# Strassen's seven products for the up projections of both token halves, with the gate products kept in HBM

## The chip, the cores and the metric

One core of a Trainium2 chip runs one program. The metric is the device time of one execution in microseconds (us); the time before is the median of three runs. The engines are named as in the profile: PE (TensorE, matmuls), DVE (VectorE), ACT (ScalarE), POOL (GpSimd) and SP (SyncE, whose queue issues all transfers here).

## The reference

Two post-norm layers over 1024 tokens of width 1024, in float32. Layer 0 has a mixer of gated MLP and sparse attention, layer 1 a convolution module; behind each comes the same kind of feed-forward part, which this change is about:

```
def conv_ffn(x, w_up, conv_w, conv_b, w_down):
    h = causal_dwconv(x @ w_up, conv_w, conv_b)
    g, u = jnp.split(h, 2, axis=-1)
    return (jax.nn.gelu(g) * u) @ w_down
...
x <- LayerNorm(alpha * x + f(x))        # behind every part
```

`w_up` is 1024 x 5632 (2816 gate and 2816 up columns), the convolution is causal with width 3, `w_down` is 2816 x 1024. Layer 1's mixer is `x @ w_in` (to 2 x 1024), a sigmoid gate, a causal depthwise convolution of width 31, LayerNorm, swish and `@ w_out`.

## The kernel before

Float32 accuracy comes from splitting each operand into a high and a low part in the fast matmul type; a product is three matmuls (`mm3`: high x low, low x high, high x high). `split` and `wload` make the parts: ACT copies the high part, POOL (for weights) or DVE subtracts it for the low one. Each weight tile of 512 KB comes on SP's queue into one of three buffers and is split into three buffers each.

The tokens are in two halves of 512 (h = 0, 1). `ffn(h, l)` does one half of layer l: 22 pairs of a gate tile and an up tile of 128 columns. `up(j)` makes one pair: for each tile eight k-chunks of three matmuls of 128 x 128 by 512 tokens; ACT takes the bias and the newest tap from PSUM, DVE the two older taps (for h = 1 also a correction from the first half's last tokens, `hal` and `cor`), ACT the gelu, POOL the product of gate and up, and the product is split again and stays in SBUF. Behind 8, 8 and 6 pairs come the down projections (`product`, tokens in rows, weights in blocks of two k-rows), which `into` adds to Z on DVE.

Python generators set the order of the program: each `yield` ends a unit of PE work of 24 matmuls (5.44 us), and `go(gen, n, rate)` emits n units and, behind each, `rate` waiting steps of the depthwise convolution's taps (`pump`). Such a tap is one DVE instruction per 128 channels and 512 tokens, 30 per tile, accumulated in one of two PSUM buffers (tag "c"). `mix` puts units of another stream behind the short steps of a norm. So `norm(0, g1)`, `conv_in(0)` and the taps of one half lie beside the other half's feed-forward units. `norm` takes the inverse root (`rsqrt`, eleven small DVE steps) for each token tile alone, transposes on PE and splits. `conv_norm` transposes, normalizes and transposes back. The framework then orders each engine's instructions by when their inputs are expected.

Of the kernel before, what the change touches and what calls it, by code (L numbers as in the profile page):

```python
# [18 lines left out]
T = 1024  # L19
# [6 lines left out]
F2W = 256  # L26

# [10 lines left out]
def trunk_kernel(ctx, tc, xt, wab, wv, w280, wst, sgub, sgulg, sgulb, pe_k, pe_v, w1k, w1v, w2k, w2v,  # L38
# [37 lines left out]
    def mm3(out_, ah, al, bh, bl, first, last):  # L76
        nc.tensor.matmul(out_, ah, bl, start=first, stop=False)  # L77
        nc.tensor.matmul(out_, al, bh, start=False, stop=False)  # L78
        nc.tensor.matmul(out_, ah, bh, start=False, stop=last)  # L79
# [40 lines left out]
    # the first two weights come in halves, between the first parts of x  # L120
# [207 lines left out]
    VT = kp.tile([128, 8, 2, 2, 128], F32R, name="VT")  # key tile, sel/win, group, (hi|lo)  # L328
# [41 lines left out]
    def product(lhs, src, kn, done, banks=None):  # L370
        # tokens in rows: blocks of two rows of weights, four token tiles side by side
# [53 lines left out]
    def late(qi):  # L425
        # the first half's output projection starts behind the last units of attention
# [18 lines left out]
    pe_.close()  # L445
    ps = es.enter_context(pool("ps1", space=PSUM))
    with pool("att") as tp:
# [4 lines left out]
        def tables_of(h, m):  # L452
# [18 lines left out]
        def front(u):  # L471
# [11 lines left out]
            # probabilities of the two heads: selected, window, compressed  # L483
# [9 lines left out]
            for e in range(2):  # L493
# [15 lines left out]
                # where the keys begin in the two banks, and how many of them the first bank takes  # L509
# [34 lines left out]
        def back(u):  # L544
# [6 lines left out]
            # transposed probabilities, and their products with the values  # L551
# [88 lines left out]
    def norm(h, gb):  # L640
# [23 lines left out]
    hal = fp.tile([128, 44, 2], F32, name="halo")  # L664
    cor = fp.tile([128, 44, 2], F32, name="cor")

    def ffn(h, l, tail=None):
        xh, xl = XT[h]
        z = Z[h]
        cw = V[f"fw{l}"].rearrange("p (m k) -> p m k", k=3)  # L670
        cb = f"fb{l}"
        if h == 1:
            cor2 = tmp("cor2")[:, :44]
            nc.vector.tensor_tensor(cor[:, :, 0], hal[:, :, 1], cw[:, :, 1], op=OP.mult)
            nc.vector.tensor_tensor(cor2, hal[:, :, 0], cw[:, :, 0], op=OP.mult)
# [30 lines left out]
        def down_last(tail):  # L706
            # the last product of all, one token tile after the other, with its weights kept
# [21 lines left out]
        def down(gi):  # L729
            j0, j1 = KG[gi]  # L730
            return product(lambda k: prod[j0 + k], lambda dh, b: wdn[l, gi * 8 + dh * 4 + b], j1 - j0,
                           into(h, gi == 0, gi == 2))

        done = 0
        for gi, (j0, j1) in enumerate(KG):
            top = min(j1 + 1, NPAIR)
            if tail and gi == 2:
                last = down_last(tail)
            while done < top:
                for _ in up(done):  # L740
                    yield
                    if tail and gi == 2 and done < 20:
# [247 lines left out]
```

## Time and profile before

| | |
|---|---|
| time, median of 3 runs | 2356.73 us (2356.02 to 2357.6) |
| span of the profiled execution, first to last instruction | 2353.9 us |
| instructions | 30312 |
| PE busy | 2299.9 us, 98% |
| DVE, ACT, POOL busy | 1318.5, 955.4, 1347.8 us |
| moved by DMA | 232.23 MB |

The span is one execution, taken by the hardware profiler; the median lies 2.8 us above it, which is around the span. Lines L61 and on are lines of the kernel. Matmuls overlap in PE, so their busy times are a union and their mean durations are longer than what each adds.

### The profile page before, as it was taken

How to read it: one execution, taken by the hardware profiler on the slowest of the kernel's cores; microseconds unless marked ns; L12 is line 12 of the kernel's file. 1: busy time of each engine (PE TensorE's matmuls, PEld its weight loads, DVE VectorE, ACT ScalarE, POOL GpSimd, SP SyncE). 2: the span in 40 equal slices, each digit the busy share in tenths (PEclk: the TensorE clock that was granted, in tenths of full speed). 3: DMA queues.
4: the chain of work that ended last, by engine and by line, in shares of the span. 5: the costliest groups of instructions: out<-in, count | busy, mean ns of one | idle time of the engine just before them, and what ended most of it. 6: DMA issues, size and time to landing. Idle time of an engine off the chain costs nothing.

```text
span 2353.9 us, 30312 instructions
## 1 busy us (share of the span) xinstructions
PE 2299.9 (98%) x10959; PEld 1915.2 (81%) x10959; DVE 1318.5 (56%) x2628; ACT 955.4 (41%) x1594; POOL 1347.8 (57%) x1277
## 2 busy tenths in 40 slices
PE   9999899999999999999999999999999999999998
PEld 7888798887788888788888887788888887888887
DVE  3532898657422223779983546789961739423325
ACT  4133998733433333333333442334243532433341
POOL 4442777554666656555566563655566664665672
PEclk9999999999999999999999999999999999999999
DMA  7053121353232232223332232233223233333240
GB/s 232 30 150 88 51 64 53 115 184 99 90 99 92 96 99 99 81 90 98 99 96 94 89 108 90 90 99 99 94 94 99 81 117 117 108 99 98 93 140 36
DMA packets 82989, 232.23 MB, mean 99 GB/s; under 512 B 10079, under 2 KB 24039, under 8 KB 82840
## 3 DMA queue, kind: packets, MB, share of 16 engines
q1 hardware_dynamic: 82840, 230.30, 30.7%
q8 instruction: 87, 1.43, 0.2%
q14 instruction: 62, 0.51, 0.1%
HBM read 213.44 MB, written 8.43 MB: 94 GB/s over the span
## 4 chain that ended last, share of the span: by engine, by line
PE 85%; DVE 11%; ACT 1%; issue 1%; DMA 1%; POOL 0%; DVEq 0%; SPq 0%; ACTq 0%; POOLq 0%
PE pu L77 13%; PE pu L79 13%; PE pu L78 13%; PE pd L77 8%; PE pd L79 8%; PE pd L78 8%; PE pt L563 2%; DVE Z L636 2%; DVE Z L637 1%; PE pca L79 1%; PE pcg L79 1%; PE pcg L77 1%; PE pca L77 1%; PE pcg L78 1%; PE pca L78 1%; PE O L571 1%
## 5 line engine op out<-in xcount | busy, mean ns | idle before, releaser
L73 POOL TENSOR_TENSOR wl<-wraw,wh 128x512 fp32r<-128x512 f32 x680 | 883.4, 1321 | 777.7 <-ACT wh L70 763.5
L77 PE MATMUL pu<-XTl,wh 128*128 128x512 f32 x1440 | 566.2, 393 | 14.2 <-DVE nw L616 4.1
L78 PE MATMUL pu<-XTh,wl 128*128 128x512 f32 x1440 | 564.5, 392 | 0.0
L79 PE MATMUL pu<-XTh,wh 128*128 128x512 f32 x1440 | 564.4, 392 | 0.0
L70 ACT ACTIVATE wh<-wraw 128x1024 fp32r<-128x1024 f32 x340 | 357.9, 1054 | 425.3 <-PE pd L79 362.7
L689 DVE SCALAR_TENSOR_TENSOR acc<-pu,vec,acc 128x511 f32<-128x511 f32 x176 | 131.7, 748 | 440.4 <-ACT acc L688 428.3
L77 PEld LDWEIGHTS pu<-XTl,wh 128*128 128x128 f32 x1440 | 272.4, 189 | 73.4 <-issue 15.2
L767 DVE SCALAR_TENSOR_TENSOR cacc<-ht,vec,cacc 128x512 f32<-128x512 f32 x464 | 318.6, 750 | 5.5 <-ACT cacc L763 3.9
L79 PEld LDWEIGHTS pu<-XTh,wh 128*128 128x128 f32 x1440 | 272.4, 189 | 56.9
L78 PEld LDWEIGHTS pu<-XTh,wl 128*128 128x128 f32 x1440 | 272.7, 189 | 56.1
L688 ACT ACTIVATE acc<-pu,vec 128x512 f32<-128x512 f32 x176 | 137.1, 779 | 423.5 <-PE pu L79 423.2
L77 PE MATMUL pd<-wl,ph 128*128 128x512 f32 x656 | 259.4, 396 | 0.8 <-DVE Z L398 0.4
L78 PE MATMUL pd<-wh,pl 128*128 128x512 f32 x656 | 258.9, 395 | 0.0
L79 PE MATMUL pd<-wh,ph 128*128 128x512 f32 x656 | 256.9, 395 | 0.0
L77 PEld LDWEIGHTS pd<-wl,ph 128*128 128x128 f32 x656 | 123.6, 188 | 31.3 <-DVE Z L398 2.0
L79 PEld LDWEIGHTS pd<-wh,ph 128*128 128x128 f32 x656 | 123.5, 188 | 28.6
L78 PEld LDWEIGHTS pd<-wh,pl 128*128 128x128 f32 x656 | 123.7, 188 | 28.4
L398 DVE TENSOR_TENSOR Z<-Z,pd 128x512 f32<-128x512 f32 x64 | 43.7, 685 | 178.9 <-PE pd L79 178.9
L690 DVE SCALAR_TENSOR_TENSOR acc<-pu,vec,acc 128x510 f32<-128x510 f32 x176 | 131.5, 747 | 4.6
L396 DVE SCALAR_TENSOR_TENSOR Z<-Z,pd 128x512 f32<-128x512 f32 x64 | 43.7, 684 | 158.4 <-PE pd L79 158.4
L699 POOL TENSOR_TENSOR acc<-acc 128x512 f32<-128x512 f32 x88 | 113.6, 1291 | 17.6 <-DVE acc L694 14.6
L63 POOL TENSOR_TENSOR pl<-acc,ph 128x512 fp32r<-128x512 f32 x88 | 113.7, 1292 | 11.9 <-ACT ph L62 9.6
(256 smaller groups left out, 3849.0 us busy)
## 6 DMA issues: line engine op xcount, KB each, us to landing
wraw<-wup SPq DMA_DIRECT2D x176, 512.0 KB, 3.4
wraw<-wdn SPq DMA_DIRECT2D x82, 512.0 KB, 3.4
wraw<-cwin SPq DMA_DIRECT2D x32, 512.0 KB, 3.4
wraw<-wout SPq DMA_DIRECT2D x16, 512.0 KB, 4.4
wraw<-cwout SPq DMA_DIRECT2D x16, 512.0 KB, 3.5
wraw<-wab SPq DMA_DIRECT2D x14, 512.0 KB, 3.8
gb<-lns SPq DMA_DIRECT2D x12, 512.0 KB, 3.6
B<-fd SPq DMA_DIRECT2D x8, 512.0 KB, 3.6
```

Source lines behind the costliest of these rows:

```text
L63: (leng or nc.vector).tensor_tensor(lo, src, hi.bitcast(F32), op=OP.subtract)
L70: nc.scalar.activation(wh[:, :n], raw[:, :n], AF.Copy)
L73: (leng or nc.gpsimd).tensor_tensor(wl[:, c], raw[:, c], wh[:, c].bitcast(F32), op=OP.subtract)
L77: nc.tensor.matmul(out_, ah, bl, start=first, stop=False)
L78: nc.tensor.matmul(out_, al, bh, start=False, stop=False)
L79: nc.tensor.matmul(out_, ah, bh, start=False, stop=last)
L563: nc.tensor.transpose(pt[:, j, e * 128:(e + 1) * 128], P[:, e, o:o + kn], ident)
L688: nc.scalar.activation(a, p, AF.Identity, scale=cw[:, mt, 2:3], bias=col(cb, mt))
L689: nc.vector.scalar_tensor_tensor(a[:, 1:], p[:, :511], cw[:, mt, 1:2], a[:, 1:], op0=OP.mult, op1=OP.add)
L690: nc.vector.scalar_tensor_tensor(a[:, 2:], p[:, :510], cw[:, mt, 0:1], a[:, 2:], op0=OP.mult, op1=OP.add)
L699: nc.gpsimd.tensor_tensor(acc[0], acc[0], acc[1], op=OP.mult)
L767: nc.vector.scalar_tensor_tensor(c[0] if k else ht[:, :H], ht[:, k:k + H], dww[:, j, k:k + 1], c[0], op0=OP.mult, op1=OP.add)
```

## The change

The up projection of a pair is taken as a 2 x 2 block product: rows are the gate tile and the up tile, the 1024 inputs are two halves of 512, and the tokens are two halves of 512. Strassen's form (in Winograd's variant) makes it from seven products of 512 inputs by 512 tokens where the plain form has eight. The sums of token blocks (T1 to T4) are made once per layer (`sums`), those of the weight blocks per pair (`prep`). `block` runs the seven products on two PSUM tiles of two banks; three of them accumulate onto banks that ACT or DVE has read in between, and DVE adds the rest. Taps, gelu and product then run over 1024 tokens.

A layer now has three stages. `up_lead` makes the first 4 pairs (layer 0) or 8 pairs (layer 1) in the old form, half by half; `up_rest` makes the second half's lead and then the other pairs by `block`; every product goes to HBM (`pd`). Then `down(0, l)` and `down(1, l)` fetch the products back, split them and run the down projections. The normalized tokens are written to HBM (`zd`) by `norm` and fetched back as Z. `norm` takes one inverse root for all four token tiles. Three of the sixteen depthwise tiles (`POOLED`) have their taps as an ACT multiplication and a POOL addition. Layer 0's second down projection and the lead tiles of layer 1 now lie beside the convolution's parts.

```
+LEAD = (4, 8)
+NP = 23
+POOLED = ((0, 3), (1, 1), (1, 3))
...
+    def mm3(out_, ah, al, bh, bl, first, last, more=False):
+        nc.tensor.matmul(out_, ah, bl, start=first, stop=False, skip_group_check=more)
+        nc.tensor.matmul(out_, al, bh, start=False, stop=False, skip_group_check=more)
...
+    keep = ctx.enter_context(pool("keep"))
+    hal = keep.tile([128, 2 * max(LEAD), 2], F32, name="halo")
+    cor = keep.tile([128, 2 * max(LEAD), 2], F32, name="cor")
+    pd = [[tc.dram_tile([128, 1024], F32, name=f"pd{l}_{j}") for j in range(NPAIR)] for l in range(2)]
+    zd = [tc.dram_tile([2, 128, 4, 1024], F32, name=f"zd{l}") for l in range(2)]
...
+    def ptile(dtype, name, w=512):
+        return fa.tile([128, w], dtype, name=name, tag="p", bufs=NP)
...
+    def norm(h, gb, keep=None):
         xh, xl = XT[h] = A("xh", F32R, name="XTh"), A("xl", F32R, name="XTl")
+        mv = fp.tile([128, 4, 2], F32, name="mv4", bufs=2)
+        for tt in range(4):
+            nc.vector.bn_aggr(mv[:, tt], ST[h][:, tt])
+        r = rsqrt(mv[:, :, 1], 4)
         for tt in range(4):
             ts = slice(tt * 128, (tt + 1) * 128)
-            (n_,) = normed(h, tt, gb)
+            n_ = Z[h][:, tt]
+            nc.vector.scalar_tensor_tensor(n_, n_, mv[:, tt, 0:1], gb[0], op0=OP.subtract, op1=OP.mult)
+            nc.vector.scalar_tensor_tensor(n_, n_, r[:, tt:tt + 1], gb[1], op0=OP.mult, op1=OP.add)
+            if keep is not None:
+                nc.sync.dma_start(keep[h, :, tt, :], n_)
...
+    bg, bgp = [], []
 
     def pump(k):
-        for _ in range(min(k, len(bg))):
-            bg.pop(0)()
+        for q, n in ((bg, k), (bgp, (k + 3) // 4)):
+            for _ in range(min(n, len(q))):
+                q.pop(0)[1]()
+    def drain(h):
+        while any(h_ == h for h_, _ in bg + bgp):
+            pump(4)
...
+    def up_lead(h, l, bank):
...
+        for j in range(LEAD[l]):
...
-            hi = fp.tile([128, 512], F32R, name="ph", tag="p", bufs=18)
-            lo = fp.tile([128, 512], F32R, name="pl", tag="p", bufs=18)
-            split(hi, lo, acc[0], nc.gpsimd)
-            prod[j] = (hi, lo)
+            nc.sync.dma_start(pd[l][j][:, h * H:(h + 1) * H], acc[0])
...
+        (x0h, x0l), (x1h, x1l) = XT[0], XT[1]
+        t1 = A("z", F32R, (128, 2, 4, 512), name="T1")
+        t2 = A("z", F32R, (128, 2, 4, 512), name="T2")
+        t3 = fp.tile([128, 2, 4, 512], F32R, name="T3")
+        t4f = []
+        def sums(k):
+            f = lambda t_, i: t_.bitcast(F32)[:, i, :]
+            b11, b12, b22 = (fp.tile([128, 512], F32, name="tv", tag="tv", bufs=3) for _ in range(3))
+            if k % 2 == 0:
+                t4f.append(tmp_("t4f"))
+            b21 = t4f[-1][:, k % 2 * 512:k % 2 * 512 + 512]
+            nc.gpsimd.tensor_tensor(b11, f(x0h, k), f(x0l, k), op=OP.add)
+            nc.vector.tensor_tensor(b12, f(x1h, k), f(x1l, k), op=OP.add)
+            nc.gpsimd.tensor_tensor(b22, f(x1h, k + 4), f(x1l, k + 4), op=OP.add)
+            nc.vector.tensor_tensor(b21, f(x0h, k + 4), f(x0l, k + 4), op=OP.add)
+            nc.vector.tensor_tensor(b22, b22, b12, op=OP.subtract)
+            nc.vector.tensor_tensor(b12, b12, b11, op=OP.subtract)
+            nc.vector.tensor_tensor(b11, b22, b11, op=OP.add)
+            nc.vector.tensor_tensor(b21, b21, b11, op=OP.subtract)
+            split(t2[:, 0, k, :], t2[:, 1, k, :], b11)
+            split(t3[:, 0, k, :], t3[:, 1, k, :], b22, nc.gpsimd)
+            split(t1[:, 0, k, :], t1[:, 1, k, :], b12)
+        lead = up_lead(1, l, lambda: psn("q", "pu", (128, 2, 512))[:, 0])
+        for i, _ in enumerate(lead):
+            if i < 4:
+                sums(i)
+        for k in range(4):
+            split(x1h[:, k, :], x1l[:, k, :], t4f[k // 2][:, k % 2 * 512:k % 2 * 512 + 512], nc.gpsimd if k % 2 else None)
+        B11, B21 = (x0h[:, :4], x0l[:, :4]), (x0h[:, 4:], x0l[:, 4:])
+        B22, T4 = (x1h[:, 4:], x1l[:, 4:]), (x1h[:, :4], x1l[:, :4])
+        T1, T2, T3 = ((t_[:, 0], t_[:, 1]) for t_ in (t1, t2, t3))
+        def prep(j):
+            ra, rb = W4(F32, name="wraw"), W4(F32, name="wraw")
+            nc.sync.dma_start(ra, wup[l, 2 * j])
+            nc.sync.dma_start(rb, wup[l, 2 * j + 1])
+            s = ua.tile([128, 1024], F32, name="ws", bufs=2)
+            lo, hi = slice(0, 512), slice(512, 1024)
+            add = lambda o, a, b, op: nc.vector.tensor_tensor(o, a, b, op=op)
+            w = {}
+            def parts(src, h_, l_, n=2):
+                nc.scalar.activation(h_, src, AF.Copy)
+                for c in (lo, hi)[:n]:
+                    nc.gpsimd.tensor_tensor(l_[:, c], src[:, c], h_[:, c].bitcast(F32), op=OP.subtract)
+                return [(h_[:, c], l_[:, c]) for c in (lo, hi)[:n]]
+            w["11"], w["12"] = parts(ra, W4(F32R, name="wh", tag="wh"), W4(F32R, name="wl", tag="wl"))
+            add(s[:, lo], rb[:, lo], rb[:, hi], OP.add)
+            add(s[:, hi], s[:, lo], ra[:, lo], OP.subtract)
+            add(rb[:, lo], ra[:, lo], rb[:, lo], OP.subtract)
+            add(ra[:, hi], ra[:, hi], s[:, hi], OP.subtract)
+            w["s1"], w["s2"] = parts(s, *(ua.tile([128, 1024], F32R, name=n, bufs=2) for n in ("sh", "sl")))
+            w["s4"], = parts(ra[:, hi], *(ua.tile([128, 512], F32R, name=n, bufs=2) for n in ("s4h", "s4l")), n=1)
+            yield w
+            w["s3"], w["22"] = parts(rb, W4(F32R, name="wh", tag="wh"), W4(F32R, name="wl", tag="wl"))
+            yield
+        def prod7(o, w, x, first=True):
+            wh, wl = w
+            xh, xl = x
+            for k in range(4):
+                s = slice(k * 128, (k + 1) * 128)
+                mm3(o, wh[:, s], wl[:, s], xh[:, k, :], xl[:, k, :], first and k == 0, k == 3, not first)
+        flat = lambda p: p.rearrange("p h t -> p (h t)")
+        def block(j, w, nxt):
+            pa, pb = (psn("q", n, (128, 2, 512)) for n in ("pa", "pb"))
+            t_, v_ = (fp.tile([128, 512], F32, name=n, tag="tv", bufs=3) for n in ("tt", "tv"))
+            add = lambda o, a, b: nc.vector.tensor_tensor(o, a, b, op=OP.add)
+            prod7(pa[:, 0], w["11"], B11)
+            prod7(pb[:, 1], w["s2"], T2)
+            nc.scalar.activation(t_, pa[:, 0], AF.Copy)
+            add(t_, t_, pb[:, 1])
+            prod7(pb[:, 0], w["s3"], T3)
+            add(v_, t_, pb[:, 0])
+            prod7(pa[:, 1], w["s1"], T1)
+            add(pb[:, 1], v_, pa[:, 1])
+            prod7(pa[:, 0], w["12"], B21, False)
+            if nxt:
+                next(nxt)
+            prod7(pb[:, 0], w["22"], T4, False)
+            add(pb[:, 0], t_, pb[:, 0])
+            prod7(pa[:, 1], w["s4"], B22, False)
+            add(pa[:, 1], t_, pa[:, 1])
+            acc = []
+            for e, p in enumerate((pa, pb)):
+                mt = 2 * j + e
+                a = tmp_("acc")
+                p = flat(p)
+                nc.scalar.activation(a, p, AF.Identity, scale=cw[:, mt, 2:3], bias=col(cb, mt))
+                nc.vector.scalar_tensor_tensor(a[:, 1:], p[:, :1023], cw[:, mt, 1:2], a[:, 1:], op0=OP.mult, op1=OP.add)
+                nc.vector.scalar_tensor_tensor(a[:, 2:], p[:, :1022], cw[:, mt, 0:1], a[:, 2:], op0=OP.mult, op1=OP.add)
+                if e == 0:
+                    nc.scalar.activation(a, a, AF.Gelu_apprx_tanh)
+                acc.append(a)
+            for c in (slice(0, 512), slice(512, 1024)):
+                nc.gpsimd.tensor_tensor(acc[0][:, c], acc[0][:, c], acc[1][:, c], op=OP.mult)
+            nc.sync.dma_start(pd[l][j], acc[0])
+        now = prep(LEAD[l])
+        w = next(now)
+        next(now)
+        for j in range(LEAD[l], NPAIR):
+            nxt = prep(j + 1) if j + 1 < NPAIR else None
+            w1 = next(nxt) if nxt else None
+            block(j, w, nxt)
+            w = w1
...
+    def down(h, l, tail=None):
+        prod = {}
+        def fetch(k):
+            raw = tmp("praw")
+            nc.sync.dma_start(raw, pd[l][k][:, h * H:(h + 1) * H])
+            prod[k] = ptile(F32R, "ph")[:, :512], ptile(F32R, "pl")[:, :512]
+            split(*prod[k], raw, nc.gpsimd)
...
+        Z[h] = A("z", F32, (128, 4, 1024), name="Z")
+        for tt in range(4):
+            nc.sync.dma_start(Z[h][:, tt, :], zd[l][h, :, tt, :])
+        ahead = 8
+        for k in range(ahead):
+            fetch(k)
...
+            for i, _ in enumerate(gen):
+                if 2 * i >= j1 - j0:
+                    for ahead in range(ahead, min(ahead + 2, NPAIR)):
+                        fetch(ahead)
+                    ahead = min(ahead + 1, NPAIR)
+                if tail and gi == 1 and 1 <= i < 7:
+                    next(lt)
+                yield
...
+            pool_ = (h, j) in POOLED
...
+                    if pool_:
+                        tp = fp.tile([128, H], F32, name="tp", bufs=2)
+                        nc.scalar.activation(tp, ht[:, k:k + H], AF.Copy, scale=dww[:, j, k:k + 1])
+                        nc.gpsimd.tensor_tensor(o, tp, c[0], op=OP.add)
...
+    mix(norm(0, g0, zd[0]), O1, 2)
     go(O1)
-    F00 = ffn(0, 0)
-    mix(norm(1, g0), F00, 1)
-    go(F00, 56)
-    F10 = ffn(1, 0)
-    go(F10, 2)
+    L0 = up_lead(0, 0, lambda: psn("u", "pu"))
+    mix(norm(1, g0, zd[0]), L0, 1)
+    go(L0)
+    fs.close()
+    up_rest(0)
...
+    D0, D1 = down(0, 0), down(1, 0)
+    go(D0, 18)
     g1 = affine(1)
+    go(D0)
+    go(D1, 1)
+    mix(norm(0, g1), D1, 1)
+    C0, C1 = conv_in(0), conv_in(1)
+    go(C0, 8, rate=5)
+    go(D1, 11, rate=6)
+    go(C0, 4, rate=5)
+    go(D1, rate=6)
+    g1 = affine(1)
+    mix(norm(1, g1), C0, 1)
+    go(C1, 10, rate=9)
+    drain(0)
+    mix(conv_norm(0), C1, [1, 1, 0, 0])
     g2 = affine(2)
+    go(conv_out(0), rate=9)
+    mix(norm(0, g2, zd[1]), C1, 1)
+    L0 = up_lead(0, 1, lambda: psn("u", "pu"))
+    go(L0, 4, rate=20)
+    drain(1)
+    mix(conv_norm(1), L0, 1)
     g2 = affine(2)
     go(conv_out(1))
+    mix(norm(1, g2, zd[1]), L0, 1)
+    go(L0)
+    fs.close()
+    up_rest(1)
...
+    D0, D1 = down(0, 1), down(1, 1, lambda tt: final(1, g3)(tt))
+    go(D0)
     g3 = affine(3)
     for tt in range(4):
+        go(D1, 2)
         final(0, g3)(tt)
+    go(D1)
```

## Rows read from the trace of the kernel before

**Rows 1.** The page, busy time of the engines with shares of the span.
```profile
PE 2299.9 (98%) x10959; PEld 1915.2 (81%) x10959; DVE 1318.5 (56%) x2628; ACT 955.4 (41%) x1594; POOL 1347.8 (57%) x1277
```

**Rows 2.** The page, DVE's busy tenths in 40 slices.
```profile
DVE  3532898657422223779983546789961739423325
```

**Rows 3.** The page, the chain that ended last, by engine.
```profile
PE 85%; DVE 11%; ACT 1%; issue 1%; DMA 1%; POOL 0%; DVEq 0%; SPq 0%; ACTq 0%; POOLq 0%
```

**Rows 4.** Timeline of PE, 24 matmuls apart: start, us, engine, line, operation.
```profile
1099.87 0.39 PE L77 MATMUL pu<-XTl,wh 128*128 128x512 f32 x1
...
1105.31 0.39 PE L77 MATMUL pu<-XTl,wh 128*128 128x512 f32 x1
```

**Rows 5.** Groups by line and shape: busy us, mean ns | idle before, releaser.
```profile
L73 POOL TENSOR_TENSOR wl<-wraw,wh 128x512 fp32r<-128x512 f32 x680 | 883.4, 1321 | 777.7 <-ACT wh L70 763.5 <-DMA flg<-flag 10.5 <-PE pn L648 3.4
L70 ACT ACTIVATE wh<-wraw 128x1024 fp32r<-128x1024 f32 x340 | 357.9, 1054 | 425.3 <-PE pd L79 362.7 <-issue 39.9 <-PE pk L79 5.9
L767 DVE SCALAR_TENSOR_TENSOR cacc<-ht,vec,cacc 128x512 f32<-128x512 f32 x464 | 318.6, 750 | 5.5 <-ACT cacc L763 3.9
...
L688 ACT ACTIVATE acc<-pu,vec 128x512 f32<-128x512 f32 x176 | 137.1, 779 | 423.5 <-PE pu L79 423.2
...
L398 DVE TENSOR_TENSOR Z<-Z,pd 128x512 f32<-128x512 f32 x64 | 43.7, 685 | 178.9 <-PE pd L79 178.9
...
L63 DVE TENSOR_TENSOR mt<-mraw,mt 128x512 fp32r<-128x512 f32 x8 | 7.7, 986 | 4.2 <-ACT mt L62 4.1
...
L63 DVE TENSOR_TENSOR vl<-vg,vh 128x512 fp32r<-128x512 f32 x8 | 5.5, 684 | 5.4 <-ACT vh L62 5.4
```

**Rows 6.** Groups of DVE from 962 to 1000 us.
```profile
L637 DVE SCALAR_TENSOR_TENSOR Z<-Z,nw,gb 128x1024 f32<-128x1024 f32 x4 | 5.1, 1281 | 0.0
```

**Rows 7.** DMA issues: count, KB each, median us to landing.
```profile
wraw<-wup SPq DMA_DIRECT2D x176, 512.0 KB, 3.4
...
mraw<-mixd SPq DMA_DIRECT2D x8, 256.0 KB, 5.3
```

**Rows 8.** Timeline of SP's queue from 40 to 80 us.
```profile
47.68 0.80 SPq L69 DMA_DIRECT2D wraw<-w1k  x2
...
75.63 0.39 SPq L234 DMA_DIRECT2D mixd<-at  x1
```

**Rows 9.** Windows: us, busy per engine (instructions), clock, DMA share, GB/s.
```profile
1070.00:1200.00 130.00, 130.00 (x570) 106.83 (x569) 125.76 (x196) 45.01 (x55) 72.23 (x61) 1.00 0.31 97
596.00:611.00 15.00, 15.00 (x61) 12.21 (x60) 5.71 (x11) 7.13 (x12) 7.61 (x6) 0.83 0.32 116
951.00:2082.00 1131.00, 1113.17 (x4961) 913.02 (x4961) 763.64 (x1363) 421.87 (x578) 662.83 (x533) 0.99 0.30 97
```

**Rows 10.** Timeline of DVE, one inverse root and what follows.
```profile
1315.28 0.15 DVE L613 TENSOR_SCALAR nw<-mv 128x1 f32<-128x1 f32 x1
...
1317.40 0.81 DVE L812 TENSOR_SCALAR nrm<-pz,mv,nw 128x512 f32<-128x512 f32 x1
```

**Rows 11.** Timeline of PE behind a gap (in brackets: idle before, releaser).
```profile
595.04 0.77 PE L77 MATMUL pu<-XTl,wh 128*128 128x512 f32 x1 [2.14 <-DVE halo L692]
...
601.15 0.40 PE L79 MATMUL pu<-XTh,wh 128*128 128x512 f32 x1
...
604.79 1.03 PE L648 MATMUL pn<-ident,Z 128*128 128x128 f32 x8
605.58 0.48 PE L77 MATMUL pu<-XTl,wh 128*128 128x512 f32 x1
```

**Rows 12.** Timeline of DVE, taps of the depthwise convolution, merged.
```profile
1159.30 12.60 DVE L767 SCALAR_TENSOR_TENSOR cacc<-ht,vec,cacc 128x512 f32<-128x512 f32 x19
...
1221.26 0.73 DVE L767 SCALAR_TENSOR_TENSOR ht<-ht,vec,cacc 128x512 f32<-128x512 f32 x1
```

**Rows 13.** Groups of DVE from 1311 to 1376 us, in conv_norm.
```profile
L812 DVE TENSOR_SCALAR nrm<-pz,mv,nw 128x512 f32<-128x512 f32 x8 | 6.1, 804 | 0.1
L806 DVE BATCH_NORM_STATS2 cst<-pz 128x6 f32<-128x512 f32 x8 | 5.4, 690 | 1.3 <-PE pz L805 1.1
```

More of the change, by code (lines that the diff above doesn't have):

```diff
@@ L74, in wload @@
         return wh, wl
[L76 to L79, printed above, removed]
+    def mm3(out_, ah, al, bh, bl, first, last, more=False):
+        nc.tensor.matmul(out_, ah, bl, start=first, stop=False, skip_group_check=more)
+        nc.tensor.matmul(out_, al, bh, start=False, stop=False, skip_group_check=more)
+        nc.tensor.matmul(out_, ah, bh, start=False, stop=last, skip_group_check=more)
     def mtile(out_, w, xh, xl, kn=8):
@@ L597, in trunk_kernel @@
     es.close()
-    fp = ctx.enter_context(pool("ffn"))
-    ps = ctx.enter_context(pool("ps2", space=PSUM))
+    keep = ctx.enter_context(pool("keep"))
[3 more added lines that the diff above has]
+    zd = [tc.dram_tile([2, 128, 4, 1024], F32, name=f"zd{l}") for l in range(2)]
+    fs = ExitStack()
+    ft = fs.enter_context(pool("fft"))
+    fa = fs.enter_context(pool("ffa"))
+    fp = fs.enter_context(pool("ffn"))
+    ps = fs.enter_context(pool("ps2", space=PSUM))
     def tmp(name, w=512, bufs=4):
-        return fp.tile([128, w], F32, name=name, tag="t", bufs=bufs)
+        return ft.tile([128, w], F32, name=name, tag="t", bufs=bufs)
+    def ptile(dtype, name, w=512):
+        return fa.tile([128, w], dtype, name=name, tag="p", bufs=NP)
     def psn(tag, name, shape=(128, 512)):
-        return ps.tile(list(shape), F32, name=name, tag=tag, bufs={"u": 2, "d": 4, "c": 2}[tag])
+        return ps.tile(list(shape), F32, name=name, tag=tag, bufs={"u": 2, "d": 4, "c": 2, "q": 4}[tag])
     def rsqrt(v, n):
@@ L699, in up, with up_rest, tmp_ @@
             nc.gpsimd.tensor_tensor(acc[0], acc[0], acc[1], op=OP.mult)
-            hi = fp.tile([128, 512], F32R, name="ph", tag="p", bufs=18)
-            lo = fp.tile([128, 512], F32R, name="pl", tag="p", bufs=18)
-            split(hi, lo, acc[0], nc.gpsimd)
-            prod[j] = (hi, lo)
+            nc.sync.dma_start(pd[l][j][:, h * H:(h + 1) * H], acc[0])
             yield
-        def down_last(tail):
+    def up_rest(l):
+        nonlocal fp, ps
+        us = ExitStack()
+        ua = us.enter_context(pool("upa"))
+        fp = us.enter_context(pool("up"))
+        ps = us.enter_context(pool("ps3", space=PSUM))
+        def tmp_(name, w=512, bufs=4):
+            return fp.tile([128, 1024], F32, name=name, tag="acc", bufs=4)
+        nonlocal tmp
+        tmp0, tmp = tmp, tmp_
+        cw = V[f"fw{l}"].rearrange("p (m k) -> p m k", k=3)
+        cb = f"fb{l}"
+        (x0h, x0l), (x1h, x1l) = XT[0], XT[1]
[100 more added lines that the diff above has]
+            w = w1
+        us.close()
+        tmp = tmp0
@@ L727, in down_last @@
                 yield
[L729 to L734, printed above, removed]
+        Z[h] = A("z", F32, (128, 4, 1024), name="Z")
[4 more added lines that the diff above has]
+            fetch(k)
+        lt = last() if tail else None
         for gi, (j0, j1) in enumerate(KG):
-            top = min(j1 + 1, NPAIR)
             if tail and gi == 2:
[L738 to L742, printed above, removed]
-                        next(last)
-                done += 1
-            yield from last if tail and gi == 2 else down(gi)
-    tails = fp.tile([128, 8, 30], F32, name="tails")
+                yield from lt
+                break
+            gen = product(lambda k: prod[j0 + k], lambda dh, b: wdn[l, gi * 8 + dh * 4 + b], j1 - j0,
+                          into(h, gi == 0, gi == 2))
+            for i, _ in enumerate(gen):
[6 more added lines that the diff above has]
+                yield
     for n_ in ("cbin", "cng", "cnb"):
@@ L766, in f @@
                 def f():
-                    nc.vector.scalar_tensor_tensor(c[0] if k else ht[:, :H], ht[:, k:k + H], dww[:, j, k:k + 1],
-                                                   c[0], op0=OP.mult, op1=OP.add)
+                    o = c[0] if k else ht[:, :H]
+                    if pool_:
+                        tp = fp.tile([128, H], F32, name="tp", bufs=2)
+                        nc.scalar.activation(tp, ht[:, k:k + H], AF.Copy, scale=dww[:, j, k:k + 1])
+                        nc.gpsimd.tensor_tensor(o, tp, c[0], op=OP.add)
+                    else:
+                        nc.vector.scalar_tensor_tensor(o, ht[:, k:k + H], dww[:, j, k:k + 1], c[0],
+                                                       op0=OP.mult, op1=OP.add)
                 return f
-            return [first] + [tap(k) for k in range(29, -1, -1)]
+            return [(h, f) for f in (first, *(tap(k) for k in range(29, -1, -1)))]
         for j in range(8):
-            ht = fp.tile([128, 30 + H], F32, name="ht", bufs=8)
+            ht = ptile(F32, "ht", 30 + H)
             p = psn("u", "pca")
@@ L788, in conv_in @@
             CV[h].append(ht)
-            bg.extend(taps(ht, j))
+            (bgp if (h, j) in POOLED else bg).extend(taps(ht, j))
             yield
@@ L843, in trunk_kernel @@
     O0 = LATE[1]
-    m1 = [[fp.tile([128, 512], F32R, name="mt", tag="p", bufs=18) for _ in range(2)] for k in range(8)]
+    m1 = [[ptile(F32R, "mt")[:, :512] for _ in range(2)] for k in range(8)]
     for _ in mixed(1, m1):
```

61 lines of the change are left out of this document (20 added, 41 removed).

## The prediction

> **What bounds the kernel now.** I read the busy shares first [rows 1]: TensorE (PE) is busy 98% of the span, no other engine more than 57%. The slices [rows 2] show VectorE (DVE) swinging from 1 to 9 tenths along the way; it is near full only around the attention and the convolution. The chain that ended last [rows 3] is 85% PE and 11% DVE. So the kernel costs, almost everywhere, its number of matmuls times what one takes of PE, and that is not their duration of 0.39. In [rows 4] a matmul starts at 1099.87 and the one 24 places on at 1105.31: 5.44/24 = 0.227 us each, since they overlap. With the duration one would overrate the saving by 1.7.
>
> **The change, part by part.**
>
> *Matmuls.* A pair (gate tile and up tile) took 2 tiles x 2 halves x 24 = 96 matmuls; it takes 7 products x 4 k-chunks x 3 = 84. 18 pairs of layer 0 and 14 of layer 1 change (the leads of 4 and 8 keep the old form): 32 x 12 = 384 x 0.227 = **87.0 us less**. Down projections, convolution and transposes keep their counts.
>
> *Inside a block.* It has 84 x 0.227 = 19.0 us of PE to hide the rest under. ACT: three copies of 1024 at 1.05, one of 512 and one read-back at 0.78 at most, two Identities and a gelu of 1024 from 1.05 to twice 0.78 each: 7.9 to 9.4 us. POOL: seven subtractions and two products at 1.32: 11.9. DVE: five adds on PSUM at 0.69, four taps over 1022 columns from 1.28 (1024 columns, in SBUF) to 2 x 0.75, four adds of weights from 0.68 to 0.99: 11.3 to 13.4 [rows 5, 6]. All are below 19.0, so I cost it at nothing; PE is the cover. The tightest hand-overs: the fifth product writes the bank that ACT must have copied and comes 8.2 us after the first has ended; the sixth and seventh each come 5.4 us after the result that DVE must have read. A block loads two weights at 3.4 us each [rows 7].
>
> A weight add has two operands in SBUF. The subtraction "vl" took 0.68 and the same shape "mt" 0.99 [rows 5], so something at times holds such an instruction up. The Trainium skill, page "SBUF — State Buffer", section "Who interferes with whom", says that a DVE instruction with two SBUF inputs and a GpSimd instruction that reads SBUF exclude each other for a whole instruction. By it each of the four adds could wait out a POOL subtraction: DVE would have up to 11.3 + 4 x 1.32 = 16.6 us, still below 19.0, and the sum stays.
>
> *Queues.* The product writes wait on SP for POOL's multiplication, and behind them stand the next weights. That would stall PE if queues kept the program's order. They don't: the loads of w1k went out at 47.68, the mixd writes that the program has before them at 75.63 [rows 8]. I cost it at nothing; without that cover see the third rival. The traffic (23 MB of products and 8 MB of norm results, each out and back, 33 MB of weights less) meets DMA engines busy 0.30 of the time [rows 9].
>
> *Norms.* One inverse root for four tiles: 11 small DVE steps, 1315.28 to 1317.40 [rows 10], once and not four times: 6 us less DVE per norm, counted below.
>
> *Starts and ends of the seven-product stages.* Layer 0's sums take 4 x 8 DVE adds and subtractions at 0.68 to 0.99, 22 to 32 us, beside 8 lead tiles x 2 x 0.75 and small steps, 16, in 43.5 us of PE; POOL has (16 + 4 + 12) x 1.32 = 42 in the same time. Either can run over by 0 to 10 us; I take 5. Layer 1 has twice the lead: nothing. At the end the next stage's first operands must be fetched (5.3 us for 256 KB [rows 7], then ACT and POOL, 2 us) into SBUF that the last block holds until its fourth product, 8.1 us before its end: 0 to 7 us, I take 2.5, twice. Together **+10**.
>
> *The convolution stretch* is where I see the money go: from the end of layer 0's first down projection (0 here) to layer 1's second lead. Before, 44 up tiles of each half lay beside the taps; most of them have left. PE's work there: 22 down units, 32 conv_in tiles and 16 lead tiles of 24 matmuls, two conv_out of 192: 2064 x 0.227 = 468 us, and 256 transposes, 8 of which took 0.79 from their start to the next matmul's [rows 11], 25: 493 us. DVE's: a tap takes 0.663 (19 in 12.60 [rows 12]; its own 0.75 [rows 5] overlaps), and 13 of 16 tiles x 30 = 390 remain on DVE.
> - PE first has five down units and the norm's transposes (30.4), then two conv_in tiles: the first taps start at 43. Three chains (the fourth tile is POOL's) take 60 us, with other steps to about 108; the next conv_in tile pair ends after six more of its kind and 11 down units: 30.4 + 21 x 5.44 + 1.4 = 146. DVE stands nearly idle for 38 us.
> - From 146 on DVE has no break until the last tap: 300 taps, 199; two norms of 4 x (2 x 1.28 + 2 x 0.68) + 3 = 18.7, 37; conv_norm(0), 4 x (2 x 0.69 + 2 x 0.80 + 2 x 0.69 + 2.3) [rows 13], 27; additions into Z with statistics, 22; conv_in, 8; eight lead tiles, 12: 305, so 451.
> - Then nothing covers: conv_norm(1), 27 and about 11 for its last tile's way over PE, ACT and POOL, to 489; what is left of conv_out (138 of 192 matmuls, 31), 520; eight lead tiles and transposes, 47: 567. The eight don't slip forward, since conv_out's first weights hold the three buffers.
>
> 567 - 493 = 74 us without PE work. The old stretch also lost some, 1131 - 1113.2 = 18 [rows 9], which goes. After a gap PE runs slowly at first: from 595.04 to 601.15 fourteen matmuls took 6.1 us where 3.2 would do [rows 11], at a granted clock of 0.83 on average from 596 to 611 [rows 9]; one such restart more is +3. Net **+59**.
>
> Sum against the profiled execution: 2353.9 - 87.0 + 10 + 59 = 2335.9 of span; the median of the runs is 2.8 above that span, so **2338 us**, rounded down. Low bound: the lead tiles do slip forward (-26) and half the 38 us hole is filled (-20): 2292. High bound: 300 taps at 0.75 (+26), the norms' steps as slow against POOL as "mt" (+5), starts and ends at twice the price (+10): 2379.
>
> **Rivals.**
> 1. *The convolution gives back little* (28 us without PE work, not 74). For it: DVE takes taps whenever it is free (97% busy from 1070 to 1200 [rows 9], all done by 1222 [rows 12]), so another order fills holes. Against: in layer 0's first down projection DVE has next to nothing to do, and that can't be caught up. 2292 to 2317.
> 2. *The other side: DVE's chain is longer and the stretch eats the gain.* Same place; a tap costs its own 0.75, or a norm waits for a PSUM buffer that a tap chain holds (30 x 0.663 = 20 us). From 19 us more on, 0.062 us per tap over 300, the kernel is no faster. Against: the spacing of 0.663 held over 19 taps in a row. 2361 to 2385.
> 3. *Queues in program order stall the blocks.* ACT's read-back would stand behind the next pair's copies, these behind DVE's weight adds, these behind the last pair's taps: add 0.7, Identity 1.2, two taps 2.6, gelu 1.1, Identity 1.2, two taps 2.6, four adds 2.8, copies 1.1 and 0.6, read-back 0.6, together 14.5 us into the block, where 10.9 is due: 3.6 x 32 = 115 us, 2453. From 0.6 us per block on it decides. Against it: [rows 8].
> 4. *The clock stays low in the stretch.* PE works there in short bursts, and each gap like the 2.1 us before 595.04 [rows 11] costs 2.9. If both conv_outs' remaining 138 matmuls ran at 0.427 (1.2 GHz) and not 0.227, that is 2 x 27 = 54 us more: 2392. The Trainium skill, page "TensorE: Matmul & The Clock Gate", section "HAM oscillation — how this bites in real kernels", tells of a kernel in which every wait for operands throws the clock back. The trace agrees as far as single gaps go; but 951 to 2082 still has 0.99 on average [rows 9], with short gaps.
>
> That the 384 matmuls go is certain from the text; that a slot stays 0.227 is likely, since their shapes are unchanged.
>
> **How the numbers follow.** Likeliest as worked out (2317 to 2358) 0.45; rival 1 0.30; rival 2 0.16; rival 3 0.05; rival 4 0.04. 0.2% is 4.7 us, about what a measurement of this kernel can tell from no change: faster is below 2352, slower above 2361. Of the likeliest case 0.36 lies below 2352 and the rest on the edge: faster 0.66, same 0.08, slower 0.26. The range of 8 in 10 leaves out rivals 3 and 4 and the ends of 1 and 2: 2292 to 2376.
>
> **What would show it.** 10575 matmuls (of 10959) at 0.227; blocks of 19.0 us without gaps, 609 us in all, DVE 60 to 70% busy in them. In the stretch DVE is full for 300 us and PE has gaps that wait for DVE, near conv_norm and the norms, 74 us together, with the granted clock below 1 behind them. Below 35 rival 1 is right, above 93 rival 2. Gaps in the blocks behind ACT's read-back mean rival 3, slots of 0.427 in conv_out rival 4. Wrong altogether would be down projections that wait for fetched products, which I cost at nothing past the start: POOL has 2.6 for weights and up to 2.6 for two fetches in a unit of 5.4.

## The result, and the profile after

The changed kernel takes 2439.93 us (median of 4 runs, 2438.01 to 2441.52) against 2356.38 us before: ratio 1.0357, 95% interval 1.0342 to 1.0371. It is slower by 84 us, where 2338 was predicted; 2440 lies above the range and above all rivals but the third. Its profiled span is 2439.8 us, 103.9 above the predicted sum.

The page after: busy time of the engines (against [rows 1]), DVE's 40 slices (against [rows 2]) and the granted clock in tenths.

```profile
PE 2252.5 (92%) x10575; PEld 1863.7 (76%) x10575; DVE 1463.7 (60%) x2440; ACT 1019.2 (42%) x1652; POOL 1504.2 (62%) x1363
...
DVE  2533998565965666411495997998576555531334
...
PEclk9999999999989999999999997986999999989999
```

The 384 matmuls are gone (10959 - 10575), but PE's busy share fell from 98% to 92%. The next view tells for whom PE waited: engine, line, tile, releaser; us in total, times, the longest.

```profile
PE pz L979 <- DVE ht L941: 36.4, 4, 22.1
PE pa L81 <- DVE acc L840: 16.7, 26, 3.8
PE pn L990 <- DVE nrm L986: 16.4, 3, 7.7
PE pd L81 <- ACT ph L65: 15.1, 2, 7.6
PE pn L673 <- DVE XTl L66: 9.6, 7, 6.2
PE pu L81 <- DVE halo L719: 7.9, 5, 2.7
PE pa L81 <- DVE pb L817: 6.5, 3, 2.7
PE pd L82 <- POOL pl L66: 5.8, 2, 4.4
PE pa L81 <- DVE acc L717: 5.6, 1, 5.6
...
PE pu L82 <- POOL wl L76: 5.1, 2, 2.8
```

Three places stand out. The convolution and the norms: `pz` and the `pn` rows, 62 us (L941 is a tap). The blocks and their start: `pa` behind the taps of a block (L840), behind an addition (L817), behind a lead tile's tap (L717), and a lead tile's `pu` behind a weight (`wl`), 34 us. The starts of the down projections, `pd` behind fetched products, 21 us.

### The profile page after: what moved, and what is told of

The parts are those of the page before. It is cut to its first block, busy times and chain, and to the rows that moved or that the text cites. A ratio compares the mean times of both kernels' runs of the same rounds, so it can differ in the third digit from the quotient of the medians.

```text
span 2439.8 us, 30086 instructions
## 1 busy us (share of the span) xinstructions
PE 2252.5 (92%) x10575; PEld 1863.7 (76%) x10575; DVE 1463.7 (60%) x2440; ACT 1019.2 (42%) x1652; POOL 1504.2 (62%) x1363
## 5 line engine op out<-in xcount | busy, mean ns | idle before, releaser
L76 POOL TENSOR_TENSOR wl<-wraw,wh 128x512 fp32r<-128x512 f32 x424 | 572.5, 1373 | 353.6 <-ACT wh L73 335.0
L73 ACT ACTIVATE wh<-wraw 128x1024 fp32r<-128x1024 f32 x212 | 223.6, 1056 | 268.5 <-PE pd L83 218.8
L941 DVE SCALAR_TENSOR_TENSOR cacc<-ht,vec,cacc 128x512 f32<-128x512 f32 x377 | 265.7, 749 | 7.7 <-ACT cacc L931 4.7
L792 POOL TENSOR_TENSOR wl<-wraw,wh 128x512 fp32r<-128x512 f32 x128 | 165.8, 1317 | 38.4 <-ACT wh L790 37.6
L81 PE MATMUL pu<-XTl,wh 128*128 128x512 f32 x416 | 165.4, 398 | 8.0 <-DVE halo L719 7.9
L82 PE MATMUL pu<-XTh,wl 128*128 128x512 f32 x416 | 164.5, 395 | 5.2 <-POOL wl L76 5.1
L83 PE MATMUL pu<-XTh,wh 128*128 128x512 f32 x416 | 164.0, 394 | 0.0
L81 PE MATMUL pa<-XTl,wh 128*128 128x512 f32 x256 | 105.1, 411 | 29.9 <-DVE acc L840 16.7
L66 POOL TENSOR_TENSOR pl<-praw,ph 128x512 fp32r<-128x512 f32 x88 | 114.1, 1319 | 26.7 <-PE pd L82 19.7
L544 POOL TENSOR_SCALAR P<-P,sm 128x64 f32<-128x64 f32 (+6 forms) x192 | 106.9, 579 | 21.7 <-DVE sm L538 12.7
L939 POOL TENSOR_TENSOR cacc<-tp,cacc 128x512 f32<-128x512 f32 x87 | 114.5, 1317 | 7.4 <-ACT tp L938 5.2
L66 DVE TENSOR_TENSOR ptl<-pt,pth 128x512 fp32r<-128x512 f32 (+1 forms) x160 | 101.0, 644 | 27.9 <-ACT pth L65 21.0
```

The costliest lines, as they stand in the source:

```text
L66: (leng or nc.vector).tensor_tensor(lo, src, hi.bitcast(F32), op=OP.subtract)
L73: nc.scalar.activation(wh[:, :n], raw[:, :n], AF.Copy)
L76: (leng or nc.gpsimd).tensor_tensor(wl[:, c], raw[:, c], wh[:, c].bitcast(F32), op=OP.subtract)
L81: nc.tensor.matmul(out_, ah, bl, start=first, stop=False, skip_group_check=more)
L82: nc.tensor.matmul(out_, al, bh, start=False, stop=False, skip_group_check=more)
L83: nc.tensor.matmul(out_, ah, bh, start=False, stop=last, skip_group_check=more)
```

## The experiments

Each is timed beside the kernel before, whose median moved by 1.5 us at most between the series (2355.2 to 2356.7), and its distance to the changed kernel (2440) is what it tells.

**The taps.** Only the first step and one tap are left of each convolution tile; the other 29 taps are left out.

```
-            return [(h, f) for f in (first, *(tap(k) for k in range(29, -1, -1)))]
+            return [(h, f) for f in (first, tap(0))]
```

> Each convolution tile keeps its first (ScalarE) step and one tap; 29 of 30 taps are left out (377 of 390 on VectorE), so the convolution is not computed. If the taps on VectorE are what PE waits for between layer 0's first down projection and layer 1's blocks, most of the 127 us without PE work there go: 2330 to 2355, idle in the stretch 15 to 35. If it is the chains of the norms and of the staging themselves (rival), the taps are hidden and the time stays above 2410.

2345.1 us: 95 us less, as the first theory had it. The stretch from the end of layer 0's first down projection to layer 1's second lead, 620 us in the changed kernel (1172 to 1792, first row), is 531 here (second row), with PE idle for 19 us and not 90, and the clock nearly full (windows; columns as in [rows 9]).

```profile
1172.00:1792.00 620.00, 529.56 (x2318) 430.20 (x2317) 485.38 (x790) 259.69 (x387) 400.49 (x325) 0.91 0.29 93
```

```profile
1166.00:1697.00 531.00, 511.70 (x2348) 420.25 (x2348) 231.65 (x418) 205.52 (x304) 294.98 (x242) 0.99 0.34 110
```

**The arithmetic.** All stages stay, but each pair of a block is made plainly.

```
-            prod7(pa[:, 0], w["11"], B11)
...
-            add(pa[:, 1], t_, pa[:, 1])
+            for e, p in enumerate((pa, pb)):
+                we = wload(wup[l, 2 * j + e])
+                mtile(p[:, 0], we, x0h, x0l)
+                mtile(p[:, 1], we, x1h, x1l)
```

> The same stages, leads, norm and product stores, but each pair of a block is computed plainly: 96 matmuls, no sums, no weight adds. If a seven-product block costs its matmuls only (as predicted), this is 87 slower than the changed kernel: 2527. If the blocks' own waits and the sums at the start of the stage cost some 45 of the 87 (theory): 2475 to 2490. If they eat it all: 2440. Against the kernel before it shows what the staging alone costs: theory +120 to +135.

2471.7 us. So the seven products bring 32 us of the 87 that their matmuls are worth: 55 us go back inside their own stages, more than the theory's 45. The stages cost the rest.

**The norm alone**, in the kernel before.

```
+        r = rsqrt(mv[:, :, 1], 4)
         for tt in range(4):
...
-            (n_,) = normed(h, tt, gb)
+            n_ = Z[h][:, tt]
```

> The kernel before with the one inverse root for four tiles alone (its two small buffers once instead of twice, for space). If VectorE's small steps are off the path there, as its busy shares say: within 0.2%, 2352 to 2358. If each norm's 6 us of VectorE stood on the path: 2356 - 36 = 2320.

2340.3 us, ratio 0.9934 (0.9922 to 0.9947): neither, but a gain of 16 us, and the fastest kernel of this study. DVE's timeline in the first half of a norm shows why; before:

```profile
586.34 1.34 DVE L617 SCALAR_TENSOR_TENSOR nw<-nw 128x1 f32<-128x1 f32 x2
...
589.11 1.25 DVE L617 SCALAR_TENSOR_TENSOR nw<-nw 128x1 f32<-128x1 f32 x1
...
590.89 0.70 DVE L618 SCALAR_TENSOR_TENSOR nw<-nw 128x1 f32<-128x1 f32 x1
...
592.11 1.27 DVE L637 SCALAR_TENSOR_TENSOR Z<-Z,nw,gb 128x1024 f32<-128x1024 f32 x1
```

(the first row is two steps), on POOL meanwhile:

```profile
588.47 3.10 POOL L73 TENSOR_TENSOR wl<-wraw,wh 128x512 fp32r<-128x512 f32 x2 [0.80 <-ACT wh L70]
```

and on DVE with one root for four tiles:

```profile
576.01 6.93 DVE L650 SCALAR_TENSOR_TENSOR Z<-Z,nw,gb 128x1024 f32<-128x1024 f32 x4
```

Before, four roots run between larger steps, a step of one column takes up to 1.25 us there (0.15 in [rows 10]; the last section shows what it waits for), and the last tile's Z is begun at 592.11. With one root all four are done by 582.94. PE's last transposes of this norm come at 604.79 in [rows 11]; here:

```profile
599.23 1.04 PE L654 MATMUL pn<-ident,Z 128*128 128x128 f32 x8
```

So 5.6 us are won by then, and 14.1 at the end of the span. The way from the kernel before to the changed one thus has three steps: -16 for the norm (2340.3), +131.3 for the stages (2471.7), -31.7 for the seven products (2439.9).

**Both at once**: plain blocks and one tap (29 taps left out).

> Plain blocks of 96 matmuls and 29 of 30 convolution taps left out, both together. If the taps' cost in the stretch is independent of the form of the blocks, this is 2471.7 - 95 = 2377 (2370 to 2383), and what is left over the kernel with the norm alone, 36 us, is two starts of down projections (13.4 each, with restarts of the clock) and little else. If taps and blocks share a limit (VectorE): below 2365 or above 2390.

2376.9 us. Taps cost 95 us whatever the form of the blocks, so of the 131 for the stages 95 hang on the taps and 36 on the rest. No run leaves the taps out of the kernel before; there PE was idle for 18 of 1131 us [rows 9], so they cost at most about that there, and most of the 95 comes with the new stages. What PE waits for at a start of the down projections, on PE and on SP's queue, in the kernel with plain blocks and all taps:

```profile
1052.37 0.39 PE L83 MATMUL pb<-XTh,wh 128*128 128x512 f32 x1
1065.69 2.05 PE L81 MATMUL pd<-wl,ph 128*128 128x512 f32 x4 [12.93 <-issue]
```

```profile
1059.98 0.33 SPq L831 DMA_DIRECT2D pd<-acc  x1
1060.36 9.42 SPq L844 DMA_DIRECT2D praw<-pd  x7
```

The fetches stand on SP behind the last block's store, which waits for its taps and product.

**The hand-over of a bank.** In the changed kernel a block's seventh product (`s4h`) starts every 19.70 us, but for the first two and the last of each layer, not every 19.04:

```profile
841.20 0.39 PE L81 MATMUL pa<-XTl,s4h 128*128 128x512 f32 x1
...
860.90 0.39 PE L81 MATMUL pa<-XTl,s4h 128*128 128x512 f32 x1
...
868.84 0.39 PE L83 MATMUL pa<-T,sh 128*128 128x512 f32 x1
869.61 0.47 PE L81 MATMUL pa<-XTl,wh 128*128 128x512 f32 x1 [0.38 <-DVE acc L840]
```

```profile
868.18 1.27 DVE L840 SCALAR_TENSOR_TENSOR acc<-pa,vec,acc 128x1022 f32<-128x1022 f32 x1
```

The matmul at 869.61 has the operands of a first or a fifth product, and only a first one waits for a tap. The next block's first product had come before this block's fifth; so this is that of the block after it, on the bank that the block which ended at 863.6 has just left. The framework has put two products, 5.4 us, between them; the second tap has read the bank only at 869.45. First, that tap is left out in all blocks (the oldest weight of the width-3 convolution):

```
-                nc.vector.scalar_tensor_tensor(a[:, 2:], p[:, :1022], cw[:, mt, 0:1], a[:, 2:], op0=OP.mult, op1=OP.add)
```

> The second of the two taps at the end of each seven-product block is left out (the oldest of the three weights of that convolution, for the block pairs only). Theory: the next block's first product is scheduled 5.4 us behind this block's last and waits for that tap to have read its bank, 0.54 us in every block, and longer in the last block; without it blocks take 19.1: 2440 - 32 x 0.54 - 3 to 6 = 2415 to 2422. Rival: the wait only moves to the other tap or to the weight sums, and blocks stay at 19.7: 2436 to 2440.

2404.2 us, 36 less, more than expected. Two blocks take 38.08, which is 19.04 each: 0.66 x 32 = 21 of the 36. The rest lies outside the blocks' spacing; among it, the last block's tail gets shorter, and with it the wait at the down projection's start (7.55 before `pd` in the changed kernel):

```profile
870.57 0.39 PE L81 MATMUL pa<-XTl,s4h 128*128 128x512 f32 x1
...
908.65 0.39 PE L81 MATMUL pa<-XTl,s4h 128*128 128x512 f32 x1
...
1027.26 2.05 PE L81 MATMUL pd<-wl,ph 128*128 128x512 f32 x4 [5.11 <-ACT ph L65]
```

Then the whole computation with the tails in the other order, the bank pair that is complete 2.7 us earlier first:

```
-            for e, p in enumerate((pa, pb)):
+            for e, p in ((1, pb), (0, pa)):
```

> The whole computation, with the two tails of a block in the other order: first the bank pair whose last product comes one product (2.7 us) earlier, then the one that the next block's first product is waiting for. If the 0.66 us per block are this hand-over (theory), that bank is free 4.4 to 5 us after the block's last product, where 5.4 are to be had: blocks of 19.1, the last block's and the second block's waits shorter by 1 to 2.5: 2408 to 2420. If the wait only changes its place: 2435 to 2441.

2423.3 us, 17 less: in the direction, a little short. Two blocks take 38.60, 19.30 each, so 0.40 of the 0.66 per block is gone, 13 us of the 17. The framework also puts the products in another order here (the seventh ones come 14.1 and 24.5 us apart by turns), so this run alone doesn't single out the tap.

```profile
856.19 0.39 PE L81 MATMUL pa<-XTl,s4h 128*128 128x512 f32 x1
...
894.79 0.39 PE L81 MATMUL pa<-XTl,s4h 128*128 128x512 f32 x1
```

**The start of layer 0's blocks.**

```
-LEAD = (4, 8)
+LEAD = (8, 8)
```

> Layer 0 leads with 8 pairs instead of 4: four pairs of the 18 go back to the plain form, 48 matmuls more (10.9) and four hand-overs of 0.65 fewer (2.6). If the sums are what stops PE at the start of layer 0's seven-product stage (6.0 and 2.0 us and a restart of the clock, theory), those gaps shrink to those of layer 1 (1.5 and 1.5) and some 9 to 12 come back: 2436 to 2440. If they are the block's own first steps: gaps as before, 2447 to 2450.

2440.2 us, unchanged: the matmuls given back (10.9 us) cost what was won, so the shorter waits at the start are worth about 8 beside the 2.6 of four hand-overs. The first block's seventh product comes at 778.3 here, at 701.8 in the changed kernel. In the 105 us around it PE is busy 98.11 and the clock 0.98; in the changed kernel (second row) 90.48 and 0.92:

```profile
731.00:836.00 105.00, 98.11 (x419) 79.26 (x419) 61.06 (x71) 39.95 (x47) 66.57 (x50) 0.98 0.26 83
```

```profile
655.00:760.00 105.00, 90.48 (x371) 72.50 (x369) 70.93 (x76) 39.06 (x47) 70.63 (x50) 0.92 0.23 76
```

**The start of the down projections.** The first eight fetches go out from ACT's queue.

```
-            nc.sync.dma_start(raw, pd[l][k][:, h * H:(h + 1) * H])
+            (nc.scalar if k < 8 else nc.sync).dma_start(raw, pd[l][k][:, h * H:(h + 1) * H])
```

> The first eight product fetches of each down projection are issued from ScalarE's queue, not from SP's, where they stand behind a weight load that waits for its buffer. If that queue makes the start of layer 0's and layer 1's first down projections late (7.9 and 2.0, 7.9 and 5.0 us of PE), 8 to 20 come back with the restarts: 2420 to 2432. If the last block's own tail on ScalarE and GpSimd, or the memory that it holds, sets it: 2436 to 2442.

2441.8 us: no gain. ACT's timeline in this kernel:

```profile
1037.68 0.83 ACTq L865 DMA_DIRECT2D praw<-pd  x2
...
1046.13 1.06 ACT L842 ACTIVATE acc<-acc 128x1024 f32<-128x1024 f32 x1 [2.76 <-DVE acc L840]
1047.09 0.61 ACT L65 ACTIVATE ph<-praw 128x512 fp32r<-128x512 f32 x1
```

The first fetches go out about when they do from SP (1038.2 there), and the first split stands on ACT right behind the last block's gelu, which waits for its taps. PE waits the same 7.55 us. So in the changed kernel SP's queue is not what PE waits for here; the last block's tail on ACT is.

**The convolution's order.** Eight queued taps are handed out behind each step of the first convolution's norm.

```
-    mix(conv_norm(0), C1, [1, 1, 0, 0])
+    for i, _ in enumerate(conv_norm(0)):
+        go(C1, [1, 1, 0, 0][i])
+        pump(8)
```

> Eight queued taps are handed out behind each of the four steps of the first convolution's norm, where the program hands out none; VectorE was idle there for 15 of the 20 us from 1500 to 1520. If that idle time is what put VectorE's last tap late (theory: the order, not VectorE's speed), 8 to 15 come back: 2425 to 2432. If taps only get between the norm's short steps, as they do in the second layer's norm of the first half (9.3 us without PE work): 2440 to 2450.

2424.1 us, 16 less, with no work taken away. DVE from 1500 to 1520 here:

```profile
1500.00:1520.00 20.00, 16.48 (x58) 12.46 (x57) 18.02 (x26) 15.79 (x28) 17.70 (x14) 0.76 0.00 1
```

and in the changed kernel, with the window in which I had DVE without a break, the hole at the end of the taps, and the first 15 us of a down projection:

```profile
1500.00:1520.00 20.00, 17.00 (x66) 13.10 (x65) 4.96 (x8) 16.63 (x33) 17.70 (x15) 0.81 0.07 25
...
1318.00:1678.00 360.00, 285.61 (x1223) 230.02 (x1222) 321.61 (x503) 155.11 (x231) 238.96 (x195) 0.88 0.25 81
...
1655.50:1677.50 22.00, 0.27 (x2) 0.00 (x0) 21.00 (x29) 0.00 (x0) 0.00 (x0) 0.50 0.08 29
1047.00:1062.00 15.00, 13.60 (x48) 10.42 (x49) 0.00 (x0) 5.01 (x9) 11.90 (x10) 0.78 0.61 210
```

**Less DVE work there, and more PE work.** Two more tiles' taps on POOL; in another kernel more leads in layer 1, eight units ahead of the last taps and two behind each step of the second convolution's norm.

```
-POOLED = ((0, 3), (1, 1), (1, 3))
+POOLED = ((0, 3), (0, 5), (1, 1), (1, 3), (1, 5))
```

```
-LEAD = (4, 8)
+LEAD = (4, 12)
...
-    go(L0, 4, rate=20)
+    go(L0, 8, rate=10)
     drain(1)
-    mix(conv_norm(1), L0, 1)
+    mix(conv_norm(1), L0, 2)
```

> Two more of the 16 convolution tiles (tile 5 of each half) do their taps on GpSimd, with ScalarE's products: VectorE has 60 taps less, 40 us at 0.663. If VectorE's taps bound the stretch (theory), 15 to 35 of that come back: 2405 to 2425. If the stretch's length is set by chains of short steps in the norms, or GpSimd becomes the bound: 2435 or more.

> Layer 1 leads with 12 pairs instead of 8, eight of their 24 first-half tiles ahead of the second convolution's last taps, two behind each step of its norm and one behind each of the last norm's. 48 matmuls more (10.9 us) and four blocks fewer. If the holes around the second convolution's norm (22.6, 5.4, 4.0, 3.4, 2.5) are there because no matmul is to be had (theory), 20 to 35 go: 2415 to 2430. If the tiles can't slip in because buffers are held: 2447 to 2451.

2430.4 and 2432.3 us: 10 and 8 less, both short of what was expected. In the first, PE then waits 14.2 us for a chain of taps on POOL:

```profile
PE pz L979 <- POOL ht L939: 14.2, 1, 14.2
```

**Four repairs at once**: tails, taps behind the norm, five tiles on POOL, twelve leads.

> The whole computation with four repairs at once: tails in the other order, eight taps behind each step of the first convolution's norm, five tiles of taps on GpSimd, twelve leading pairs in layer 1. Alone the last three gave 16, 10 and 8 us, partly out of the same hole of 22.6, so together some 20 to 28, and the tails 20 to 30: 2382 to 2400. If the rest of the loss is the stages themselves (theory), it stays above the kernel before (2356) all the same. Below 2356 it would be mostly a matter of order.

2411.4 us, ratio 1.0238 (1.0223 to 1.0253): 29 less where the four alone add up to 50, and short of the expected 40 to 58. What holds PE at the starts of the down projections stays (`pd`, first row), and so does what holds it in the convolution's norms, mostly the first: `pn` and `pd` behind `nrm`.

```profile
PE pd L81 <- issue: 14.2, 2, 7.1
PE pn L990 <- DVE nrm L996: 11.7, 3, 8.6
...
PE pd L81 <- DVE nrm L986: 11.2, 2, 6.2
PE pn L990 <- DVE nrm L986: 8.7, 1, 8.7
```

## Why the prediction was wrong

The span exceeds the predicted sum by 104 us: 50 in the convolution stretch, 21 in the hand-overs of banks, and some 33, a remainder, at the starts and ends of the stages and all else.

- **Matmuls, -87.0**: right. The count is as given, and in blocks without the wait a slot stays 0.227 (84 x 0.227 = 19.04).
- **"Inside a block ... I cost it at nothing; PE is the cover"**: this step failed. The engines do have the time (DVE is busy 195 of the 336 us from 700 to 1036, row below), but I took the hand-overs from the order of the program, where the tightest was 5.4 us after one DVE addition. In the framework's order a first product is due 5.4 us after a block's last, where an addition, an Identity and three taps take 5.8. That is 0.65 x 32 = 21 us, shown by leaving the tap out and, for 13 us of it, by the other order. The size, 0.65 per block, is the 0.6 from which I had the third rival decide; the mechanism is another.
- **Starts, 5**: failed. A block's first bank is a lead tile's, whose taps wait among the sums (5.6 us on L717), and the first two and the last block wait more. The rest of the 55 us that the seven products lose, some 34, I put down to these and the clock's restarts, less what plain blocks wait longer for `pd`; this is a remainder, and only the 8 us at layer 0's start are shown by a run. Longer leads there take the waits away at the same price.
- **Ends, 2.5 twice**: failed; 7.6 + 1.4 and 7.6 + 4.4 us of waits, and PE then runs slowly (1047 to 1062: granted clock 0.78). I saw the SBUF that the last block holds, not its tail of 8 us, behind which the first split stands on ACT. In the blocks queues did not stall PE, as said; at the ends the third rival's mechanism, a step that stands in a queue behind the last block's, is real. The Trainium skill, page "TensorE: Matmul & The Clock Gate", section "HAM oscillation — how this bites in real kernels", tells of a kernel in which every wait for operands throws the clock back; the trace agrees for the long waits (the 0.78 stands behind 7.6 us of idle time) but not for the short ones: with 0.4 us of waiting per block the clock is 0.99 from 700 to 1036.

```profile
700.00:1036.00 336.00, 324.22 (x1399) 263.36 (x1398) 195.33 (x213) 127.17 (x133) 195.30 (x149) 0.99 0.28 93
```

- **The convolution stretch, +59**: the right place and kind (DVE's work without PE's beside it), too small, and the largest miss. 567 us were predicted, 620 came, 127 of them beyond the 493 of PE's work where I had 74. PE is idle for 90 of the 127; in the other 37 its own work goes more slowly, 529.6 us at a mean granted clock of 0.91, which I had priced at one restart, 3 us. So the stretch came out the second rival's way and beyond its price, though PE's idle time alone lies just under the 93 that I had set for it; the low clock is the fourth rival's, at less than its price. "From 146 on DVE has no break" is the step that failed: the last tap was due 451 us into the stretch (at 1623) and ends at 1678. From 1318 to 1678 DVE works 321.6 us, 16 more than the 305 of the sum, and is idle for 38. Of these, 15 lie in one window in which the program hands out no taps, and the last tile's 28 taps run late and alone. That handing them out earlier brings 16 us shows order as a cause; that 40 us less of DVE bring 10 shows that its speed is not all of it. How the rest divides among the norms' short steps and the clock isn't settled.
- **The norms, counted only in DVE's chain**: failed in the other direction. They were on PE's path; alone they give 16 us. Of DVE's time the roots' small steps take 109.9 us before and 53.0 with one root per norm: 9.5 less for each of the six norms, not 6.

So the sum of terms was -16 for the norms (not seen as such), +131 for the stages (95 of it by the taps; 64 predicted with the ends), -32 for the seven products (82 predicted with the start).

## What to carry to other kernels

Count cover by stage: matmuls that lie beside a long chain of another engine are worth less than their time when taken away, and moving them costs that chain in full. Take a hand-over of a bank from the order that the scheduler makes, and ask at each seam between stages what of the last block's tail stands ahead of the next stage's first operand on each queue. When a change is a bundle, time its smallest part alone: here only the norm was worth having, and the kernel before with it is the best version.

## What was not expected of the hardware

A step of one column on DVE can cost eight times its 0.15 us, and its neighbours on DVE aren't the reason: POOL is. Of the 324 steps of the roots with two operands in the kernel before (L616 to L618), the 227 that no POOL instruction overlaps take at most 0.16 us. Of the 97 others 58 take 0.47 to 1.29, and each of the 58 ends within 0.02 us of a POOL instruction's end: 590.36 and 591.59 in the rows of the norm, where POOL's two subtractions end at 590.35 and 591.57. The 72 first steps with one operand (L613, L614) take at most 0.16, though 51 of them run beside POOL. A chain of taps that has DVE to itself is no faster than two that take turns, but slower: 28 taps took 22.13 us, 0.79 each, against 0.663 in [rows 12].

```profile
1654.94 22.13 DVE L941 SCALAR_TENSOR_TENSOR cacc<-ht,vec,cacc 128x512 f32<-128x512 f32 x28
...
873.26 1.67 DVE L786 TENSOR_TENSOR ws<-ws,wraw 128x512 f32<-128x512 f32 x1
874.85 0.68 DVE L786 TENSOR_TENSOR wraw<-wraw 128x512 f32<-128x512 f32 x1
```

The last two rows are weight sums of a block, the first beside POOL's product of gate and up (871.38 to 874.38), the second behind it. These sums and the roots' steps agree with the rule of the Trainium skill, page "SBUF — State Buffer", section "Who interferes with whom", which the prediction weighed for the sums alone. There it was not on the path, since blocks without the tap take 19.04 with the sums in them; in the norms, which were on it, such waits make up part of what four roots cost.
